# First feed-forward output product by seven quarter products, with the later weights' low halves alone rounded ahead and stored

## The chip, the cores and the metric

The kernel runs on one core of a Trainium2 chip. A core has a matrix engine (TensorE, PE in the profile, with PEld for its weight loads), two elementwise engines (VectorE, DVE; ScalarE, ACT), GpSimd (POOL), SyncE (SP) and 16 DMA engines, which are fed here by the queues of SP and of POOL. The engines run side by side and wait for each other by semaphores; each of them works off its own instructions in order. The metric is the device time in microseconds of one execution, as the median of several runs; less is better.

## The reference

A two-layer trunk over 512 tokens of width 1024, in float32:

```python
for layer in range(2):
    if layer == 0:   # state-space group and stick-breaking attention
        mix = concat(s5_mixer(u), attention(q, k, v)) @ mix_w_out + mix_b_out
    else:            # GLU, causal depthwise convolution (31 taps), layer norm, silu
        mix = conformer_conv(x, ...)
    x = layer_norm(4**0.25 * x + mix, ln1_g[layer], ln1_b[layer])
    ffn = square(relu(x @ ffn_w1[layer] + ffn_b1[layer])) @ ffn_w2[layer] + ffn_b2[layer]
    x = layer_norm(4**0.25 * x + ffn, ln2_g[layer], ln2_b[layer])
```

`ffn_w1` is 1024 x 4096 and `ffn_w2` 4096 x 1024: 32 tiles of 128 hidden features. The change is in layer 0's feed-forward, and in when the weights of what follows are prepared: the convolution's two pointwise products (`pw1`, 16 column tiles; `pw2`, 8) and the first six column tiles of layer 1's `ffn_w1`, 30 units of 128 columns in all.

## The kernel before

**Products.** TensorE multiplies in a rounded float format (`F32R`). To keep float32's precision every operand is split: `hi` is the value rounded (an ACT copy), `lo` the rest (`src - hi`, a DVE subtraction). A product is three matmuls: hi·hi, hi·lo, lo·hi (`gemm`, line 252). Activations lie feature by token: `X[0..7]`, each 128 features by 512 tokens, is the residual.

**Weights.** The class `Weights` (line 60) holds a list of units. `next()` (154) hands out the next one and first prepares as many as `ahead` tells: `fetch` (72) loads the raw block on SP's queue into one of two `raw` buffers, then lines 112 and 113 make `hi` and `lo` in one of the rotating slots. If `fence` is set, both are put behind an instruction of the layer norm. Where a stretch's pools are closed and others opened, the function `turn` (1322) does it, at a given unit.

**Layer 0's feed-forward** (1123) runs in four blocks of eight hidden tiles. `ffn1` (1080) makes the hidden tiles: 24 matmuls of 512 columns (`f`), relu on ACT, square on DVE, split. `accum` (844) multiplies by the block's `ffn_w2`: for each of eight output tiles 8 x 3 matmuls of 512 columns (`acf`), added to `X[j]`. The first six hidden tiles are computed half by half around the layer norm (`Lead`, `fl`). The fourth block's output product is the `Tail` (1008): 256 tokens at a time (`tlb`), so that the layer norm of one half lies under the product of the other. `tail_norm_lead` (1066) strings these together: tail, norm, then the first products of what follows (the lead; `pl` for the convolution).

**Kept units.** Between these products `W.keep` (142) prepares the 30 later units in full, raw load, `hi` and `lo`, and stores both to DRAM (`kepth`, `keptl`, SP's queue). In the convolution and its tail a unit of kind `split` (94) is just two loads on POOL's queue, `hi` and `lo`, with no compute engine.

**The convolution** (1134 to 1316) has its order written out by hand: `CONV_ORDER` lists steps (`g2`: GLU of tile 2, ending in the sigmoid `csg` on ACT and the gated input `hp` on DVE; `v`: taps on DVE; `p`: taps on PE; `M`, `Q`, `n`: norm). `in_order` (1225) chains all PE, DVE and ACT instructions that a step traces. Elsewhere the compiler orders each engine's instructions, by priority and by the times it expects.

**Layer 1's feed-forward** already uses seven products in place of eight for each 2 x 2 block product: blocks of six hidden tiles, `pair` (1369) turns two hidden tiles into seven combinations, `operand` (128) makes the seven combinations of the four quarters of `ffn_w2` (tiles `quad`, loaded by `load_quads`, 120), and `seven` (1386) runs the products (`s`), 512 wide because the residual is turned to token by feature there (`residual`, 1339). Its last block of eight is an ordinary product.

Of the kernel before, what the change touches and what calls it, by code (L numbers as in the profile page):

```python
# [16 lines left out]
P = 128  # L17
# [22 lines left out]
FFN_BLOCKS = ((8, 8, 8, 8), (6, 6, 6, 6, 8))  # L40
# [7 lines left out]
KEEP_FROM = 8  # L48
# [11 lines left out]
class Weights:  # L60


    def __init__(self, tc, ahead):
        self.tc, self.nc, self.ahead = tc, tc.nc, ahead
        self.slots, self.units, self.raw, self.urgent, self.fence, self.hold = [], [], None, True, None, False
        self.done, self.got, self.chunk, self.ready, self.kept = 0, 0, {}, {}, {}
        self.turn, self.quads, self.base = None, {}, 0
# [19 lines left out]
    def _prep(self, n):  # L87
        nc = self.nc
        while self.done < min(n, len(self.units)):
            key, src, nk, ncol, off, width = self.units[self.done]  # L90
            if self.turn and self.done == self.turn[0]:
                self.turn[1]()
            pool, s = self.slots[(self.done - self.base) % len(self.slots)]
            if key[0] == "split":
                w = tuple(pool.tile([P, nk, ncol], F32R, tag=f"w{x}{s}", name=f"w{x}{self.done}", bufs=1) for x in ("hi", "lo"))
                for x, d in zip(w, self.kept[key[1]]):
                    nc.gpsimd.dma_start(x, d)  # L97
                self.ready[self.done] = w
                self.done += 1
                continue  # L100
# [5 lines left out]
            hi = pool.tile([P, nk, ncol], F32R, tag=f"whi{s}", name=f"whi{self.done}", bufs=1)  # L106
            lo = pool.tile([P, nk, ncol], F32R, tag=f"wlo{s}", name=f"wlo{self.done}", bufs=1)
# [3 lines left out]
            else:  # L111
                i0 = nc.scalar.copy(hi, raw).ins  # L112
                i1 = nc.vector.tensor_sub(lo, raw, hi.bitcast(F32)).ins  # L113
            if self.fence:
                self.tc.add_manual_dep(i0, self.fence[0], NOSYNC, reason="behind the layer norm")
                self.tc.add_manual_dep(i1, self.fence[1], NOSYNC, reason="behind the layer norm")
# [24 lines left out]

    def keep(self, i):

        w = self.next()
        self.kept[i] = tuple(self.tc.dram_tile([P, *w[0].shape[1:]], F32, name=f"kept{x}{i}") for x in "hl")
        for x, d in zip(w, self.kept[i]):
            self.nc.sync.dma_start(d, x.bitcast(F32))
# [51 lines left out]
def kernel(ctx: ExitStack, tc: tile.TileContext, a: dict, out: bass.AP):  # L199
# [13 lines left out]
    X = [const([P, T], f"X{j}") for j in range(KT)]  # L213
# [49 lines left out]
    wst = ExitStack()  # L263
    wpool = wst.enter_context(tc.tile_pool(name="mw", bufs=1))
# [600 lines left out]
    wp2 = wst.enter_context(tc.tile_pool(name="w2", bufs=1))  # L865
    hst = ExitStack()
    hid = hst.enter_context(tc.tile_pool(name="hid", bufs=1, side="right"))
# [11 lines left out]
    def hpage(name, dt=F32R, w=T):  # L879
        return hid.tile([P, PAD + T + 2], dt, tag="hid", name=name, bufs=16)[:, :w]  # L880

    def tmp(name, dt=F32):
        return hid.tile([P, T], dt, tag="tmp", name=name, bufs=8)
# [6 lines left out]
    for j in range(0, D, 128):  # L890
        later += units_of("pw1", a["conv_w_pw1"][0], 0, 8, [j], 256)
        later += units_of("pw1", a["conv_w_pw1"][0], 0, 8, [D + j], 256)
    later += units_of("pw2", a["conv_w_pw2"][0], 0, 8, range(0, D, 128), 256)
    later += units_of("f1l", a["ffn_w1"][1], 0, 8, range(0, LEAD * P, 128), 256)

    kept = [k for j in range(0, 16, 4) for k in (j, j + 2, j + 1, j + 3)] + list(range(16, 24 + LEAD))
    keep_at, n = {}, 0
    for layer in range(2):
        if layer:
            units += [(("split", i), None, 8, 128, 0, 0) for i in range(24 + LEAD)]  # L900
            at_turn = len(W.units) + len(units)
        k0 = 0
        for nb in FFN_BLOCKS[layer]:
            if layer:
                units += units_of("f11", a["ffn_w1"][1], 0, 8, range(max(k0, LEAD) * P, (k0 + nb) * P, 128), 128)
                if nb == NB:
                    units += [(("quad", k0, i), None, nb // 2, T, 0, 0) for i in ORDER7]
                else:
                    for c in (0, T):
                        for k, n_ in ((0, 3), (3, 3), (6, 2)):  # L910
                            src = a["ffn_w2"][1][(k0 + k) * P : (k0 + k + n_) * P, c : c + T].rearrange("(k p) n -> p k n", p=P)
                            units.append((("f21", k0 + k, c), src, n_, T, 0, T))
                k0 += nb
                continue
            for m in range(k0, k0 + nb, 4):
                units += units_of("f10", a["ffn_w1"][0], 0, 8, range(m * P, min(m + 4, k0 + nb) * P, 128), 256)
                if m >= KEEP_FROM:
                    keep_at["f", m + 3] = kept[n : n + 2]
                    units += [later[i] for i in kept[n : n + 2]]
                    n += 2  # L920
            for j in range(0, KT, 4):
                units += units_of("f20", a["ffn_w2"][0], k0, nb, range(j * P, (j + 4) * P, 128), 256)
                if k0 + nb < 32:
                    m = 4 if j else 2
# [590 lines left out]
```

## Time and profile before

| | us |
|---|---|
| median of 3 runs (1159.39 to 1162.86) | 1160.79 |
| the profiled execution | 1164.9 |
| its span, first to last instruction | 1163.2 |

The mean granted TensorE clock was 0.994 of full. Durations in the text come from the profiled execution. The page's second part shows how its engines are used over time, in 40 slices of 29 us; each digit is a share in tenths:

```profile
PE   9989989999999999999999999999999999999997
DVE  7999865578645645645647699988695958588337
ACT  7857759435524524523513231364673536263530
DMA  9621212150878778788617634156024151515211
```

Layer 0's feed-forward lies in slices 11 to 20, the convolution in 22 to 26, layer 1's feed-forward from 30 on. In the views below, a row of instructions names engine, line, operation, the tile written and the tiles read (without buffer numbers), then count, busy time and mean duration. Matmul durations overlap, as they are pipelined; the distance from one start to the next tells how fast they run.

### The profile page before, as it was taken

To read this page: it belongs to the slowest core of one execution; us is meant where nothing else is said; L and a number is where in the kernel's file an instruction comes from. 1 tells how busy PE (TensorE), PEld (TensorE's weight loads), DVE (VectorE), ACT (ScalarE), POOL (GpSimd) and SP (SyncE) were. 2 spreads that over 40 slices of the span, in tenths; PEclk is the share of its full clock that TensorE was granted. 3 is DMA by queue.
4 is the path that set the end of the run, shared out by engine and by line. 5 is a ranking of instruction groups with operands and counts; after the bars stand their busy time and mean duration, and the time that the engine had idled before them with its cause. 6 is when DMAs were issued, how large, how long until landed. Compare 5 with 4: busy or idle time off the path is not lost.

```text
span 1163.2 us, 17835 instructions
## 1 busy us (share of the span) xinstructions
PE 1133.7 (97%) x7156; PEld 948.5 (82%) x7156; DVE 820.6 (71%) x1401; ACT 550.0 (47%) x838; POOL 70.2 (6%) x125
## 2 busy tenths in 40 slices
PE   9989989999999999999999999999999999999997
PEld 7777767799888888888899867689988888888885
DVE  7999865578645645645647699988695958588337
ACT  7857759435524524523513231364673536263530
POOL 1022221000000000000002211002000000000000
PEclk9999989999999999999999999999999999999999
DMA  9621212150878778788617634156024151515211
GB/s 204 173 63 50 74 56 74 55 181 14 267 244 289 250 273 282 267 268 274 217 46 245 226 137 146 39 170 227 4 82 135 50 151 44 172 35 156 65 54 73
DMA packets 145907, 169.59 MB, mean 146 GB/s; under 512 B 13922, under 2 KB 119138, under 8 KB 145824
## 3 DMA queue, kind: packets, MB, share of 16 engines
q1 hardware_dynamic: 137024, 136.96, 37.1%
q0 software_dynamic: 8640, 31.46, 8.0%
q8 instruction: 56, 0.92, 0.3%
q14 instruction: 27, 0.22, 0.1%
q10 hardware_dynamic: 160, 0.03, 0.0%
HBM read 132.12 MB, written 35.65 MB: 144 GB/s over the span
## 4 chain that ended last, share of the span: by engine, by line
PE 78%; DMA 6%; DVE 6%; ACT 5%; issue 2%; SPq 2%; POOL 1%; DVEq 0%; ACTq 0%
PE f L258 20%; PE acf L258 10%; PE s L1400 10%; DMA raw<-in_ffn_w_dram 4%; PE tld L258 4%; PE h L1445 4%; PE tlb L258 4%; PE fl L258 3%; PE pv L258 3%; PE cw L1174 3%; PE pg L258 3%; PE tla L258 2%; PE acmo L258 2%; DVE wlo L113 2%; PE pl L258 2%
## 5 line engine op out<-in xcount | busy, mean ns | idle before, releaser
L112 ACT CAST whi<-raw 128x1024 fp32r<-128x1024 f32 (+1 forms) x150 | 156.6, 1061 | 259.1 <-PE acf L258 66.3
L113 DVE TENSOR_TENSOR wlo<-raw,whi 128x1024 fp32r<-128x1024 f32 (+1 forms) x150 | 183.6, 1236 | 122.1 <-ACT whi L112 122.1
L258 PE MATMUL f<-xah,whi 128*128 128x512 f32 x208 | 81.0, 390 | 0.0
L258 PE MATMUL f<-xal,whi 128*128 128x512 f32 x208 | 81.0, 389 | 0.0
L258 PE MATMUL f<-xah,wlo 128*128 128x512 f32 x208 | 80.9, 389 | 0.0
L258 PE MATMUL f<-xdh,whi 128*128 128x512 f32 x208 | 80.9, 389 | 0.0
L258 PE MATMUL f<-xdl,whi 128*128 128x512 f32 x208 | 80.9, 389 | 0.0
L258 PE MATMUL f<-xdh,wlo 128*128 128x512 f32 x208 | 80.9, 389 | 0.0
L258 PE MATMUL acf<-hl,whi 128*128 128x512 f32 x192 | 75.8, 395 | 0.1
L258 PE MATMUL acf<-hh,wlo 128*128 128x512 f32 x192 | 75.7, 394 | 0.0
L258 PE MATMUL acf<-hh,whi 128*128 128x512 f32 x192 | 75.3, 392 | 0.0
L1400 PE MATMUL s<-whi,al 128*128 128x512 f32 x168 | 65.0, 390 | 0.0
L1400 PE MATMUL s<-wlo,ah 128*128 128x512 f32 x168 | 64.9, 390 | 0.0
L1400 PE MATMUL s<-whi,ah 128*128 128x512 f32 x168 | 64.5, 392 | 0.0
L113 DVE TENSOR_TENSOR wlo<-quad,whi 128x1536 fp32r<-128x1536 f32 x28 | 49.1, 1754 | 7.6 <-ACT whi L112 7.5
L391 DVE SCALAR_TENSOR_TENSOR cy<-hp,wdw,cy 128x512 f32<-128x512 f32 (+1 forms) x75 | 49.5, 660 | 0.5 <-ACT cy L187 0.5
L112 ACT CAST whi<-quad 128x1536 fp32r<-128x1536 f32 x28 | 41.0, 1483 | 17.2 <-PE f L258 8.0
L97 POOL DMA_DIRECT2D whi<-kepth x30 | 16.0, 535 | 547.6 <-PE tlb L258 386.7
L258 PEld LDWEIGHTS f<-xdh,whi 128*128 128x128 f32 x208 | 39.0, 188 | 8.1
L258 PEld LDWEIGHTS f<-xah,wlo 128*128 128x128 f32 x208 | 39.0, 188 | 8.1
L258 PEld LDWEIGHTS f<-xah,whi 128*128 128x128 f32 x208 | 39.0, 188 | 8.1
L258 PEld LDWEIGHTS f<-xdl,whi 128*128 128x128 f32 x208 | 39.0, 188 | 8.1
(647 smaller groups left out, 3064.4 us busy)
## 6 DMA issues: line engine op xcount, KB each, us to landing
raw<-in_ffn_w_dram SPq DMA_DIRECT2D x35, 1024.0 KB, 6.0
kepth<-whi SPq DMA_DIRECT2D x30, 512.0 KB, 4.4
keptl<-wlo SPq DMA_DIRECT2D x30, 512.0 KB, 9.5
whi<-kepth POOLq DMA_DIRECT2D x30, 512.0 KB, 3.6
wlo<-keptl POOLq DMA_DIRECT2D x30, 512.0 KB, 4.4
raw<-in_ffn_w_dram SPq DMA_DIRECT2D x28, 512.0 KB, 4.0
raw<-in_conv_w_pw_dram SPq DMA_DIRECT2D x12, 1024.0 KB, 6.7
quad<-in_ffn_w_dram SPq DMA_DIRECT2D x16, 768.0 KB, 4.6
```

The costliest lines, as they stand in the source:

```text
L97: nc.gpsimd.dma_start(x, d)
L112: i0 = nc.scalar.copy(hi, raw).ins
L113: i1 = nc.vector.tensor_sub(lo, raw, hi.bitcast(F32)).ins
L258: ins = PE.matmul(ps[:, c0:c1], u[:, k, ksl], v[:, c0:c1], start=start and k == 0 and i == 0, stop=stop and k == n - 1 and i == 2).ins
L391: V.scalar_tensor_tensor(o, x, s, y, op0=op0, op1=op1)
L1174: PE.matmul(cps[j, c0][g][C, :], Ds[j][t // 16][R, t % 16, :], hps[j][R, t + c0 : t + c1], start=t < 4, stop=t >= n - 4, tile_position=(R. ...
L1400: PE.matmul(ps, u, v[:, p, :], start=chain == i and p == 0 and n_ == 0, stop=p == len(As) - 1 and n_ == 2, skip_group_check=True)
L1445: PE.matmul(ps, u, v, start=k == 0 and i == 0, stop=k == nb_last - 1 and i == 2)
```

## The change

- **Layer 0's output product.** The first 24 hidden tiles run in four blocks of six with layer 1's scheme: `pair`, `load_quads`, `operand`, and a new `seven_by_feature`. Its results stay feature by token: a quarter (two feature tiles by 256 tokens) takes two matmuls of 256 columns where layer 1 has one of 512. Product 1 gathers in two pages `R1` over all blocks. The last eight hidden tiles are computed as before; their output weights are requested between them and the first four put into the memory of the quarters (`places`).
- **Residual.** `X` becomes one tile, is scaled ahead by eight ACT passes with its bias, and the tail only adds. Squares are taken on ACT.
- **Kept units.** `half_units` takes each later unit in two halves: load on POOL's queue into a page, ACT copy, DVE subtraction in place in the loaded page, store of the low half alone on POOL's queue. Each step first issues the load of the half two steps on. There are 60 steps: one per product, one per projection (none in the first block's, two each in the last block, one each from the seventh).
- **Later units.** A `split` unit is now a raw load on SP's queue, an ACT copy for `hi` (under the fence if one is set) and a load of `lo` on POOL's queue.
- **Pools.** Three turns (into layer 0's quarters, back to plain slots, into layer 1's quarters) reopen all pools in given orders; the tail's norm takes its temporaries from the 24 pages.

```diff
-FFN_BLOCKS = ((8, 8, 8, 8), (6, 6, 6, 6, 8))
+FFN_BLOCKS = (6, 6, 6, 6, 8)
...
-            if key[0] == "split":
-                w = tuple(pool.tile([P, nk, ncol], F32R, tag=f"w{x}{s}", name=f"w{x}{self.done}", bufs=1) for x in ("hi", "lo"))
-                for x, d in zip(w, self.kept[key[1]]):
-                    nc.gpsimd.dma_start(x, d)
...
                 i0 = nc.scalar.copy(hi, raw).ins
-                i1 = nc.vector.tensor_sub(lo, raw, hi.bitcast(F32)).ins
+                if key[0] == "split":
+                    i1 = nc.gpsimd.dma_start(lo, self.kept[key[1]]).ins
+                else:
+                    i1 = nc.vector.tensor_sub(lo, raw, hi.bitcast(F32)).ins
...
+        def load(n):
+            if n < 2 * n_kept:
+                (w, c), h = later[n // 2], n % 2
+                raws[n] = page(f"kr{n}")
+                G.dma_start(raws[n].bitcast(F32).rearrange("p (k n) -> p k n", k=4), w[4 * h * P : 4 * (h + 1) * P, c : c + P].rearrange("(k p) n -> p k n", p=P))
+
+        load(0)
+        load(1)
+        for n in range(2 * n_kept):
+            load(n + 2)
+            hi, raw = page(f"kh{n}"), raws.pop(n)
+            S.copy(hi, raw.bitcast(F32))
+            V.tensor_sub(raw, raw.bitcast(F32), hi.bitcast(F32))
+            G.dma_start(W.kept[n // 2][:, 4 * (n % 2) : 4 * (n % 2) + 4, :], raw.bitcast(F32).rearrange("p (k n) -> p k n", k=4))
+            yield
...
+    ORDERS = ("s1 s2 raw s3 a1 s4 a2 a0 q w", "s1 s2 raw w a1 s4 a2 b q s3 a0")
...
+    def seven_by_feature(k0, As, first, bi):
+        bank, opened = {}, None
+        for n, i in enumerate(ORDER7):
+            wh, wl = W.next()
+            chain = CHAIN.get(i, i)
+            for b in range(2):
+                if chain == i:
+                    bank[i, b] = nps(f"z{k0}{i}{b}")
+                ps = bank[chain, b]
+                for d in range(2):
+                    c = slice((2 * b + d) * P, (2 * b + d + 1) * P)
+                    for p, (ah, al) in enumerate(As):
+                        uh, ul = ah[:, PLACE[i]], al[:, PLACE[i]]
+                        for n_, (u, v) in enumerate(((wh, uh), (wh, ul), (wl, uh))):
+                            opens = chain == i and p == 0 and n_ == 0
+                            ins = PE.matmul(ps[:, d * H : (d + 1) * H], u[:, p, c], v, start=opens and d == 0,
+                                            stop=p == len(As) - 1 and n_ == 2, skip_group_check=True).ins
...
+                    tt(x, x, halves(ps), ALU.add)
+            keep()
...
+    for bi, nb in enumerate(FFN_BLOCKS[:-1]):
+        if bi:
+            W.load_quads(k0, a["ffn_w2"][0], k0, nb)
+        As = []
+        for m in range(k0, k0 + nb, 2):
+            As.append(pair(0, m, xs, first[m : m + 2] if bi == 0 else None, keep if bi else None))
+        seven_by_feature(k0, As, bi == 0, bi)
+        k0 += nb
+    hs, ws = [], []
+    for i in range(FFN_BLOCKS[-1]):
...
+        if i < 4:
+            ws.append(W.next())
+        x = region(i // 2, i % 2)
+        tt(x, x, halves(R1[i % 2]), ALU.add)
+        keep(2 - (i > 5))
```

More of the change, by code (lines that the diff above doesn't have):

```diff
@@ L47 @@
 ONE_SUM = "bd"
-KEEP_FROM = 8
 AHEAD = (5, 4)
@@ new lines, in plain, with in_quads @@
+    def plain():
+        wst[0].close()
+        wst[0] = ExitStack()
+        p = opened("tmp raw one hid four two three".split())
+        room.update(tmp=p["tmp"], hid=p["hid"], bufs=12)
+        W.slots, W.count, W.raw, W.ahead = [], 0, p["raw"], 5
+        for x, n in (("three", 3), ("two", 2), ("one", 1), ("four", 3)):
+            W.add_slots(p[x], n)
+    def in_quads(e):
+        return lambda n: tuple(f1["w"].tile([P, 8, P], F32R, tag=f"quad{e}{f}", name=f"w2{f}{n}", bufs=1) for f in range(2))
@@ L1121, in taps @@
         tt(mask, mask, ident[:, 96:], ALU.add)
[L1123 to L1131 removed]
+        yield
+    for j in range(KT):
+        act(X[j], X[j], AF.Identity, bias=rb[1][:, j : j + 1], scale=ALPHA)
```

301 lines of the change are left out of this document (167 added, 134 removed).

## The prediction

> **What bounds the kernel now.** I read the page first: engine totals, then the chain that ended last.
>
> ```profile
> PE 1133.7 (97%) x7156; PEld 948.5 (82%) x7156; DVE 820.6 (71%) x1401; ACT 550.0 (47%) x838; POOL 70.2 (6%) x125
> ...
> PE 78%; DMA 6%; DVE 6%; ACT 5%; issue 2%; SPq 2%; POOL 1%; DVEq 0%; ACTq 0%
> PE f L258 20%; PE acf L258 10%; PE s L1400 10%; DMA raw<-in_ffn_w_dram 4%; PE tld L258 4%; PE h L1445 4%; PE tlb L258 4%; PE fl L258 3%; PE pv L258 3%; PE cw L1174 3%; PE pg L258 3%; PE tla L258 2%; PE acmo L258 2%; DVE wlo L113 2%; PE pl L258 2%
> ```
>
> TensorE leads, and `acf`, the first layer's output product outside its last block, is a tenth of the chain. An average hides stages, so next the busy times by stretch: the first feed-forward (301.5 to 577.7), its tail (to 625.6), the convolution (650 to 764).
>
> ```profile
> core 0: us, PE busy (x) PEld busy (x) DVE busy (x) ACT busy (x) POOL busy (x), PEclk, DMA share, GB/s
> 301.50:577.70 276.20, 276.11 (x1211) 225.82 (x1210) 148.53 (x165) 113.79 (x134) 0.00 (x0) 1.00 0.79 270
> 577.70:625.60 47.90, 46.96 (x390) 46.56 (x389) 29.43 (x68) 9.98 (x22) 7.55 (x14) 1.00 0.41 140
> 650.00:764.00 114.00, 110.36 (x1609) 80.63 (x1611) 106.05 (x198) 37.48 (x71) 13.73 (x26) 1.00 0.41 137
> ```
>
> In the first stretch PE never rests, while DVE works 54% and ACT 41%: there only TensorE work counts, and DVE or ACT work saved buys nothing. In the convolution PE (97%) and DVE (93%) both bind, so a wait put on either one is paid.
>
> **Term 1, the product itself.** The column after the length is PE's busy time of `acf` alone; below it starts of 512-wide and of 256-wide matmuls.
>
> ```profile
> 301.00:578.00 277.00, 134.12 (x576) 108.05 (x576) 16.47 (x24) 1.00 0.79 270
> ...
> 577.72 0.28 PE L258 MATMUL tlb<-hh,whi 128*128 128x256 f32 x1
> ...
> 578.55 0.28 PE L258 MATMUL tlb<-hl,whi 128*128 128x256 f32 x1
> ...
> 577.00:626.00 49.00, 46.91 (x384) 46.20 (x384) 7.34 (x16) 1.00 0.41 140
> ...
> 854.00:1069.00 215.00, 115.88 (x504) 94.06 (x504) 35.70 (x54) 1.35 (x2) 1.00 0.36 109
> ```
>
> Removed: 24 hidden tiles x 8 output tiles x 3 = 576 matmuls in 134.1 us, 0.233 each. Added: 4 blocks x 7 products x 3 pairs x 3 parts x 4 quarter tiles (b, d) = 1008 matmuls, 256 wide, because the layer stays feature by token. The two `tlb` starts lie seven steps apart: 0.83/7 = 0.1186 us. The whole `tlb`, waits included, gives 46.91/384 = 0.1222 (row two). I take 0.120, nearer to the undisturbed steps: 121.0 us, a gain of **13.1 us** (ends 14.6 and 10.9). The second layer does the same seven products 512 wide, 504 in 115.9 us (row three); the narrow form costs about 5 us more than that.
>
> The Trainium skill, "TensorE: Matmul & The Clock Gate", section "Back-to-back issue gap", has N/2.4 + 2.5 ns, 216 and 109 ns; by it the gain would be 576 x 0.216 - 1008 x 0.109 = 14.5 us. The trace has 233 and 119, so I keep the rows.
>
> **Term 2, cover inside the blocks.** Layer 1 already runs this pattern. Its product phase, projection phase and last block:
>
> ```profile
> 883.50:916.10 32.60, 32.60 (x145) 26.99 (x144) 21.02 (x23) 17.09 (x20) 0.00 (x0) 1.00 0.22 62
> 916.10:945.00 28.90, 28.90 (x128) 23.55 (x127) 24.65 (x27) 11.95 (x12) 0.00 (x0) 1.00 0.51 149
> ...
> 1068.00:1111.00 43.00, 43.00 (x192) 35.59 (x191) 17.00 (x17) 22.00 (x29) 0.00 (x0) 1.00 0.32 103
> ...
> L248 ACT CAST hh<-fr 128x512 fp32r<-128x512 f32 x28 | 17.3, 619 | 24.7 <-DVE fr L387 24.7
> ...
> L249 DVE TENSOR_TENSOR hl<-fr,hh 128x512 fp32r<-128x512 f32 x27 | 18.6, 689 | 11.7 <-ACT hh L248 11.7
> ```
>
> Each of the 60 kept halves adds one 512-wide ACT copy (0.62) and one DVE subtraction (0.69). A product phase gets seven: DVE 24.65 + 4.8 = 29.5 of 252 x 0.120 = 30.2 us; ACT 16.3. A projection phase gets six: DVE 25.2 of 32.6; ACT 20.8. So it fits, with nothing to spare in the product phase; a lag is buffered by three prepared weights and six PSUM banks, and drains in the projection phase. I cost it at 0.5; without that cover DVE would set the phase, at 10% over some 2 us a block, 9 in all. Residual scaling (eight ACT passes), squares and the operands' differences lie under the same cover, as they do in layer 1.
>
> **Start of block 0.** Layer 1 covers the first quarter weights with its transposes, which layer 0 lacks:
>
> ```profile
> L1346 PE MATMUL xt<-ident,X 128*128 128x128 f32 x32 | 3.8, 274 | 0.0
> ...
> L113 DVE TENSOR_TENSOR wlo<-quad,whi 128x1536 fp32r<-128x1536 f32 x28 | 49.1, 1754 | 7.6 <-ACT whi L112 7.5
> ...
> L112 ACT CAST whi<-quad 128x1536 fp32r<-128x1536 f32 x28 | 41.0, 1483 | 17.2 <-PE f L258 8.0
> ```
>
> Slot s1 opens on memory that the fifth and sixth lead weights hold; the sixth is read until 301.5. Its high half lies under the fifth, free 2.9 us sooner, so the cast (1.48) is out in time and the subtraction (1.75) comes after 301.5. Until then PE has 16 products of high weights from two finished pairs, 1.9 us. Between 0 and 3.2; I take **1.5**.
>
> **The last block.** Here layer 0 has what layer 1 has not: 8 projection and 8 output weights plus 14 halves in 8 x 5.44 = 43.5 us.
>
> ```profile
> L112 ACT CAST whi<-raw 128x1024 fp32r<-128x1024 f32 x81 | 83.1, 1049 | 122.0 <-PE acf L258 66.3 <-DMA raw<-in_ffn_w_dram 33.8 <-DMA raw<-in_conv_w_pw_dram 11.8
> ...
> q1 hardware_dynamic: 32440, 27.21, 36.2%
> ...
> q1 hardware_dynamic: 51331, 74.57, 78.4%
> ```
>
> ACT: 22.0 + 8 x 1.05 + 14 x 0.62 = 39 us at most; DVE 17 + 8 x 1.22 + 14 x 0.69 = 36. DMA: 16 x 0.524 + 14 x 0.524 = 15.7 MB. The queue rows are of 860 to 1110 and of 301 to 580: 27.21 MB in 36.2% of 250 us is 301 GB/s with 512-byte rows, 74.57 MB in 78.4% of 279 us is 341 with wider ones. Four output weights (2.1 MB) may land during the tail, so 13.6 MB, 40 to 45 us. All three are close to the block's length. Halves are two steps ahead, here only 5.4 us, and six free pages carry loads, stores and activations. A late load holds ACT's queue, behind it the relu, and with two projection banks PE. From 0 to 8 (all 15.7 MB at 301 GB/s is 52 us); I take **2.5**.
>
> The second norm: five of the later weights are cast before its lead; the three or so that fall among its squares and outputs add 1.05 each to ACT. PE has the second half of the tail meanwhile; before, only this was left over:
>
> ```profile
> PE pl L258 <- ACT xbh L187: 0.3, 1, 0.3
> ```
>
> 0 to 3, I take **0.5**.
>
> **The convolution.** A later weight used to need no compute engine; now it needs an ACT cast, and `in_order` nails ACT's order there. At step `g2`, two requests with five ahead put the casts of units 6 to 10 in front of tile 2's sigmoid `csg`.
>
> ```profile
> 651.74 0.71 ACT L187 ACTIVATE cz<-hp,wdw 128x512 f32<-128x512 f32 x1
> 661.18 0.69 ACT L193 ACTIVATE csg<-pg,PV 128x512 f32<-128x512 f32 x1 [8.74 <-PE pg L258]
> ...
> 659.21 0.08 DVE L1157 MEMSET hp<- 128x30 f32 x1
> 661.91 0.75 DVE L391 SCALAR_TENSOR_TENSOR hp<-pv,PV,csg 128x512 f32<-128x512 f32 x1 [2.62 <-ACT csg L193]
> ...
> raw<-in_ffn_w_dram SPq DMA_DIRECT2D x26, 512.0 KB, 4.0
> ```
>
> Only two raw buffers exist. From 652.4: units 6, 7 are there (cast to 654.5); unit 8's load starts at 653.5 and takes 4.0 (last row), 9 follows 1.0 later; casts to 659.7; unit 10's load starts at 658.7, its cast ends at 663.9. The sigmoid moves from 661.2 to 663.9, and DVE, already waiting there, waits 2.7 us more. Queued behind the casts on ACT are `csg`, then the start of tile 1's taps; behind DVE's wait all later taps, up to the sums of the convolution's norm. DVE's few gaps (about 1 us until 752) absorb little: **2.0**, from 0 (units landing early) to 6 (loads slowed to 6 us by the low halves). From `g3` on each step needs two casts in 11 us, hidden.
>
> The second layer's tail gets nine casts, 9.5 us, on an ACT that works about half of it: **0.5** (0 to 3). Not paid: the old 30 full casts and subtractions and the old 31 MB of stores, which the first stretch hid. Layer 1's blocks keep their operations.
>
> **Sum.** -13.1 + 0.5 + 1.5 + 2.5 + 0.5 + 2.0 + 0.5 = -5.6 us. The profiled execution took 1164.9 (span 1163.2 plus 1.7): 1159.3. The three runs' median is 1160.8, 4.1 lower: **1155**.
>
> **Rivals.**
> *All hidden.* The compiler puts low-priority copies into ACT's 23 us of idle in the tail, and nothing waits: -13.1 + 0.5 = 1148. For it: layer 1 loses almost nothing at its phase changes. Against: ACT's order in the convolution is fixed. Chance 0.13.
> *Given back.* Last block 5, block 0 3, convolution 4, others 2: +14, net about +1, 1161. For it: the tight shares above. Chance 0.23.
> *Slower: the halves' loads set the pace.* POOL issues them in order with the stores.
>
> ```profile
> L97 POOL DMA_DIRECT2D wlo<-keptl x24 | 12.9, 537 | 0.2 <-issue 0.2
> ```
>
> That is a load of 128 rows of 4 KB; a half has 512 rows of 512 B, unseen on this queue: between 0.54 and four times that, 2.1 us. At 2.1, loads and stores take 14 x 2.7 = 37 us of POOL in the last block, and a load needs about 2.1 + 4 to land, over the 5.4 us of two steps. It decides where the issue exceeds about 1.5 us and the stores do not free pages in time: then each ACT copy waits 0.3 to 1 us, some 20 of them in the product phases and all in the last block, 34 x 0.7 = 24 us; 1155 + 24 - 2.5 = 1176. Against: two steps are 8.6 us in product phases. Chance 0.20.
> The Trainium skill, "DMA: Bandwidth & Descriptors", section "Measured (HBM→SBUF, 128 partitions, SWDGE, issued from GpSimd)", asks for at least 1 MiB per transfer. Its fit in "Anatomy of one DMA", 2.0 us plus bytes/436e3, estimates 2.6 us per half, which would be in time; no run here shows such a half.
>
> **Chances.** Forecast 1149 to 1159: 0.44; all hidden 0.13; given back 0.23; slower 0.20. A measurement tells 0.3% (3.5 us) from no change: 1157.3 and 1164.3. Most of the forecast (0.42) and all hidden fall below: faster 0.55; same 0.24, mostly given back; slower 0.21. The range, 1147 to 1168, leaves out the far end of the slower case and a little below.
>
> **What would show it.** Term 1: 1008 matmuls at L-lines of `seven_by_feature`, about 121 us; over 124 refutes it. Block 0: PE idle before its first low-weight product. Last block: its eight projections longer than 43.5 us, with ACT waiting for DMA. Convolution: tile 2's `csg` near 664 less the time gained before it, DVE idle in front of it. Wrong from the start if 256-wide matmuls run slower beside 200 GB/s of transfers than in the tails.

## The result and the profile after

| | before | after |
|---|---|---|
| median of the runs, us | 1160.88 | 1203.56 (1197.36 to 1205.13) |
| profiled execution / its span, us | 1164.9 / 1163.2 | 1203.2 / 1201.5 |

The ratio is 1.0357, with a 95% interval of 1.0317 to 1.0396: slower by 3.6%, where 0.5% faster was forecast. From the page of the changed kernel, its engine totals, PE and the granted clock by slices, and the chain that ended last:

```profile
PE 1144.3 (95%) x7588; PEld 973.1 (81%) x7588; DVE 898.1 (75%) x1505; ACT 629.7 (52%) x944; POOL 128.0 (11%) x215
...
PE   9889999999998989899999999999999999999997
...
PEclk9989999999899998999999999999999999999999
...
PE 55%; DVE 10%; DMA 8%; issue 7%; ACT 6%; POOL 3%; SPq 0%; DVEq 0%; POOLq 0%; ACTq 0%
```

TensorE's share of the chain fell from 78% to 55%, although it has more matmuls. In slices 11 to 20, where PE had only nines, three are eights now, and so are two of the clock's. DVE (75%) and ACT (52%) are far from full, so the time is in waits. Measured from the start of one tile's work to the start of the next, in microseconds of the one profiled execution of each kernel:

| stretch | before | after | forecast change | measured change |
|---|---|---|---|---|
| blocks of the first feed-forward (end of `fl` to first `tlb`) | 276.1 | 299.8 | -8.6 | **+23.7** |
| its tail | 47.8 | 48.2 | 0 | +0.4 |
| lead of the convolution (`pl`) | 24.7 | 29.9 | +0.5 | **+5.2** |
| convolution | 114.3 | 115.9 | +2.0 | +1.6 |
| second layer's tail, to the first `fl` on its norm | 51.2 | 56.2 | +0.5 | **+5.0** |
| second feed-forward, from its first transpose to the first `h` | 260.3 | 264.6 | 0 | +4.3 |
| all else (mixer, leads, end) | 388.8 | 386.9 | 0 | -1.9 |

What TensorE, ACT and POOL waited for in the blocks (the largest rows of the view of waits; in total, times, longest):

```profile
PE f L254 <- ACT q L182: 12.0, 4, 3.4
PE z L1239 <- ACT ah L1120: 4.7, 3, 2.7
```
```profile
ACT kh L911 <- DMA kr<-in_conv_w_pw_dram: 30.7, 14, 4.7
...
ACT kh L911 <- DMA kept<-kr: 22.0, 14, 3.5
```
```profile
POOL kr L904 <- DMA kept<-kr: 54.0, 23, 5.0
```

Read from below: POOL's loads of halves wait for stores to land, because the page they want is still being stored; ACT's rounding copies (`kh`) wait for those loads, or for a page themselves; TensorE waits for the relu (`q`) and the combinations (`ah`) that ACT has not done. All rows of TensorE in the blocks sum to 21.2 us, where the kernel before had none, and stretches at half clock (last section) cost 11.9 us more. Less the 13.1 us that the product gains, that is 20.0 of the 23.7. One such moment, on ACT and on TensorE:

```profile
362.88 0.61 ACT L911 CAST kh<-kr 128x512 fp32r<-128x512 f32 x1
367.00 0.62 ACT L911 CAST kh<-kr 128x512 fp32r<-128x512 f32 x1 [3.50 <-DMA kept<-kr]
367.52 1.47 ACT L110 CAST whi<-quad 128x1536 fp32r<-128x1536 f32 x1
368.90 0.68 ACT L182 ACTIVATE q<-f,PV 128x512 f32<-128x512 f32 x1
```
```profile
366.49 0.39 PE L254 MATMUL f<-xah,wlo 128*128 128x512 f32 x1
369.63 0.51 PE L254 MATMUL f<-xah,whi 128*128 128x512 f32 x1 [2.75 <-ACT q L182]
```

The copy waits 3.50 us for a page; the relu, two places behind it, comes at 368.90, and TensorE, with both projection banks full, stands for 2.75 us.

Where the copies run is the second thing to see. Busy time of the copies alone (line 911), by phase. The first row is the projections of the second block; the rows behind the gap are projections and products of the third block, then of the fourth; the last row is the last block.

```profile
core 0: us, ACT busy (x), PEclk, DMA share, GB/s
...
340.30:375.90 35.60, 6.79 (x11) 0.95 0.71 221
...
407.80:448.80 41.00, 7.43 (x12) 0.96 0.75 225
448.80:484.60 35.80, 3.72 (x6) 0.90 0.60 192
484.60:522.30 37.70, 3.08 (x5) 0.95 0.53 167
522.30:553.90 31.60, 0.00 (x0) 1.00 0.21 61
553.90:597.80 43.90, 7.96 (x13) 1.00 0.84 250
```

The diff traces six copies in each projection phase and seven in each product phase. The compiler, which orders ACT here, pulled copies ahead: 11 (one straddles the edge) and 12 in the first two projection phases, none in the last product phase. Such a phase needs 32.7 us for the 144 matmuls of its six hidden tiles. The first took 35.6 us with 10 starts, although nine of its matmuls (2.0 us) had run ahead among the first block's products; the second took 41.0 with 12. That is about 3.5 us for each half.

### The profile page after: what moved, and what is told of

It is laid out like the page before. It is cut to its first block, busy times and chain, and to the rows that moved or that the text cites. A ratio compares the mean times of both kernels' runs of the same rounds, so it can differ in the third digit from the quotient of the medians.

```text
span 1201.5 us, 19145 instructions
## 1 busy us (share of the span) xinstructions
PE 1144.3 (95%) x7588; PEld 973.1 (81%) x7588; DVE 898.1 (75%) x1505; ACT 629.7 (52%) x944; POOL 128.0 (11%) x215
## 4 chain that ended last, share of the span: by engine, by line
PE 55%; DVE 10%; DMA 8%; issue 7%; ACT 6%; POOL 3%; SPq 0%; DVEq 0%; POOLq 0%; ACTq 0%
PE f L254 13%; PE s L1507 10%; PE fl L254 4%; PE z L1239 4%; PE tld L254 4%; PE h L1552 4%; DMA raw<-in_conv_w_pw_dram 2%; DMA raw<-in_ffn_w_dram 2%; PE tlb L254 2%; PE cw L1327 2%; PE tla L254 2%; ACT whi L110 2%; DVE cy L388 2%; PE acmo L254 2%; DVE wlo L114 2%
## 5 line engine op out<-in xcount | busy, mean ns | idle before, releaser
L110 ACT CAST whi<-raw 128x1024 fp32r<-128x1024 f32 (+1 forms) x122 | 128.8, 1062 | 201.9 <-PE s L1507 47.8
L114 DVE TENSOR_TENSOR wlo<-raw,whi 128x1024 fp32r<-128x1024 f32 (+1 forms) x92 | 114.5, 1247 | 85.7 <-ACT whi L110 85.6
L114 DVE TENSOR_TENSOR wlo<-quad,whi 128x1536 fp32r<-128x1536 f32 x56 | 98.1, 1754 | 10.0 <-ACT whi L110 9.1
L1239 PE MATMUL z<-ah,whi 128*128 128x256 f32 x336 | 96.1, 294 | 8.4 <-ACT ah L1120 4.7
L110 ACT CAST whi<-quad 128x1536 fp32r<-128x1536 f32 x56 | 82.2, 1481 | 37.6 <-PE z L1239 15.1
L1239 PE MATMUL z<-al,whi 128*128 128x256 f32 x336 | 97.1, 291 | 1.0 <-DVE al L1121 0.9
L1239 PE MATMUL z<-ah,wlo 128*128 128x256 f32 x336 | 96.5, 290 | 0.0
L1239 PEld LDWEIGHTS z<-ah,whi 128*128 128x128 f32 x336 | 66.1, 200 | 10.2 <-ACT ah L1120 5.5
L911 ACT CAST kh<-kr 128x512 fp32r<-128x512 f32 x60 | 37.0, 617 | 70.8 <-DMA kr<-in_conv_w_pw_dram 30.7
L912 DVE TENSOR_TENSOR kr<-kr,kh 128x512 fp32r<-128x512 f32 x60 | 41.3, 688 | 37.7 <-ACT kh L911 37.7
L1239 PEld LDWEIGHTS z<-al,whi 128*128 128x128 f32 x336 | 66.9, 199 | 1.7 <-DVE al L1121 1.6
L1239 PEld LDWEIGHTS z<-ah,wlo 128*128 128x128 f32 x336 | 66.9, 200 | 0.0
L1121 DVE TENSOR_TENSOR al<-q,ah 128x768 fp32r<-128x768 f32 (+1 forms) x48 | 52.2, 1089 | 12.2 <-ACT ah L1120 12.2
```

What stands on the lines that cost most here:

```text
L911: S.copy(hi, raw.bitcast(F32))
L912: V.tensor_sub(raw, raw.bitcast(F32), hi.bitcast(F32))
L1121: V.tensor_sub(lo, src, hi.bitcast(F32))
L1239: ins = PE.matmul(ps[:, d * H : (d + 1) * H], u[:, p, c], v, start=opens and d == 0, stop=p == len(As) - 1 and n_ == 2, skip_group_check=T ...
```

## The experiments

Each is the changed kernel with the edit shown (the last two change the kernel before); times are medians, the ratio is to the kernel before. The length of a stretch is that of one profiled execution: `best_a`, which holds the edit of `store_sp` and one more, came out 3.9 us longer there, so differences of a few microseconds between two versions are not sure.

**Parts alone.** `no_halves` takes the 60 steps out:

```diff
-            next(half_unit, None)
+            (one store in all; no load, copy or subtraction)
```


> Leaves out the 60 half steps (load, copy, subtraction, store); every later unit's low half is read from one block of DRAM written once. Theory A (the half steps hold ACT's queue, PE waits and its clock is halved after each wait): the four blocks and the last block, 299.7 us in the changed kernel from the end of the lead to the first tail product, fall to 264 to 270, and the kernel to 1167 to 1175. Rival B (the seven products 256 wide, their operands and the 512 KB loads are slow by themselves): the stretch stays above 288 and the kernel above 1190.

Measured 1177.41 us, ratio 1.0134 (1.0112 to 1.0157), blocks 274.3: most of the way to theory A, but 4 us short of its range. The halves cost 25.5 us of the blocks: TensorE's waits there fall from 21.2 to 5.2 us and what the half clock takes from 11.9 to 3.4, 24.5 together, so a third of the price is the clock. By phase, without and with the halves (the nine matmuls that ran ahead counted with their projections): first products 36.8 and 39.3; projections 32.7, 32.7, 32.7 and 37.6, 41.0, 37.7; later products 31.6, 31.6, 31.8 and 31.9, 35.8, 31.6; last block 43.5 and 43.9. So 13 of the 25.5 us lie in the two projection phases with the bunches and 12 in three phases next to them. In the last of these three, the fourth block's projections, copies wait 9.9 us for loads; in the third block's products it is a wait of 2.73 us for `ah`, around which TensorE had half its clock for 6.8 us. Almost nothing lies in the last block, where I had put it.

`no_store` leaves out the halves' stores (but the first unit's):

```diff
-            G.dma_start(W.kept[n // 2]..., raw...)
+            if n < 2: G.dma_start(W.kept[0]..., raw...)
```


> Leaves out the stores of the low halves but for the first two; loads, copies and subtractions stay. Theory A1 (pages are held until a store has landed, and copies and loads wait for pages): ACT's 22 us and POOL's 54 us of waiting for stores go, the stretch of 299.7 us falls to 275 to 285, the kernel to 1180 to 1190. Theory A2 (the loads themselves, two steps ahead, land too late, or the copies and subtractions are too much for ACT and DVE): the stretch stays at 293 or more, the kernel above 1196.

1189.21 us, 1.0241 (1.0205 to 1.0277), blocks 284.8, the upper edge of the first range. 15 of the 25.5 us come from stores, which hold pages; with pages freed at once, 15 or 16 copies fit into a projection phase of 33 to 35 us, 2.2 us each.

`hi_by_dma` loads the later units' raw blocks straight into the place of their high parts, with no cast, and `whole_units` keeps whole units as before in place of halves:

```diff
-    hi = S.copy(raw);  lo = load(kept)
+    hi = load(raw block, not rounded);  lo = load(kept)            # hi_by_dma
-    60 halves by pages
+    30 whole units by the weight slots, hi and lo stored on SP's queue   # whole_units
```


> A later unit's high half is loaded raw into its slot by POOL's queue, so its rounding on ACT is left out; all else as in the changed kernel. Theory C (casts that wait for raw loads hold ACT's queue in the second norm, in the convolution and in the second tail): the lead after the second norm falls from 29.9 to 25, the convolution from 116.0 to 114.5, the second layer's tail from 56.2 to 51.5; the kernel to 1190 to 1194. Rival D (temporaries in pages and the new order of the pools do it): all three stay within 1 us, the kernel within 3 us of 1203.6.

> Only the first part of the change: seven quarter products in layer 0; the later units are prepared whole in the weight slots, both halves stored by SP's queue and loaded by POOL's, as before the change, 30 of them between the products at every second step. Theories A and C: blocks 264 to 274 us, lead, convolution and second tail as before the change, the kernel 1150 to 1162, which would beat 1160.9 or equal it. Rivals B and D: 1180 or more.

`hi_by_dma`: 1194.45 us, 1.0289 (1.0259 to 1.0318); lead 24.7, convolution 114.0, second tail 49.9: theory C. The casts of the later units cost 5.2 + 1.9 + 6.3 = 13.4 us; 6.7 come back at the start of the second feed-forward, where the transposes now wait. Why they do was not followed. `whole_units`: 1197.25, 1.0299 (1.0269 to 1.0329); blocks and tail 347.0 against 348.0 after and 323.9 before. The 1150 to 1162 of theories A and C did not come. Lead and second tail are back (24.7 and 50.9), but the old way of keeping does no better beside the seven products: TensorE waits 14.0 us there for the casts and low parts of weights (`whi`, `wlo`). So queue and pages of the halves are not the only way to lose these 24 us; what else this version lacks was not followed. What a cast did in the second norm, on ACT in the changed kernel, and then a window of 25 us on TensorE's lead in `hi_by_dma` (busy time of PE, PEld, DVE, ACT, POOL, then granted clock, DMA share and GB/s):

```profile
639.63 1.05 ACT L110 CAST whi<-raw 128x1024 fp32r<-128x1024 f32 x1 [8.08 <-DMA raw<-in_conv_w_pw_dram]
640.59 0.47 ACT L188 ACTIVATE rb<-vpb,cb 128x256 f32<-128x256 f32 x1
```
```profile
646.00:671.00 25.00, 24.74 (x194) 24.06 (x193) 14.95 (x38) 10.68 (x22) 9.66 (x14) 1.00 1.37 269
```

The third cast stands ahead of the norm's reciprocal root and waits 8.08 us for a load. Its own 1.05 us, which I had counted, is the small part.

**The product by itself.** `product_only` joins `no_halves` and `hi_by_dma`; `product_pairs` also changes the order within each block's first product:

```diff
-    for b: for d: for each of three pairs
+    for the first two pairs over all b, d; then the third pair over all b, d     # first product only
```


> Left out: the rounding and storing of the later weights' low halves; later units load high and low parts as they are kept, with no cast (so the later products' numbers are meaningless). What stays of the change is the seven products, the early scaling and the pools. Theory (the product pays little even alone): no_halves gave 1177.4 with the blocks at 274.3, 1.8 less than before; taking the casts away gave back 5.2 in the convolution's lead, 1.9 in the convolution and 6.3 in the second layer's tail (run hi_by_dma against after). So 1177.4 - 13.4 = 1164, and 1171 if the transposes at the start of the second feed-forward wait as they did in hi_by_dma; stretch of the blocks 272 to 276. Rival (the prediction's first term is all gained once nothing else is added): blocks 263 to 265, time 1148 to 1154.

> product_only with the first product of each block taking two pairs over all quarter tiles before the third. Left out as there: rounding and storing of the later low halves and the casts of the later units. Theory M (the third pair's low part, awaited 0.9 us in each block, and the low clock after it are what is left): the 3.5 us of waits for al and 1 us for ah go, blocks 268 to 271, time 1162 to 1166. Rival N (the wait moves to the next weights): blocks 273 to 275, time 1167 to 1170. In neither case is the predicted gain of 13 there: before's blocks take 276.1.

1168.49 us, 1.0066 (1.0049 to 1.0084), blocks 274.1; and 1166.00, 1.0058 (1.0037 to 1.0079), blocks 271.1. TensorE's largest row of waits in the blocks, first of `product_only`, then of `product_pairs` (whose other two rows are 0.3 and 0.2):

```profile
PE z L1250 <- DVE al L1132: 3.5, 4, 0.9
```
```profile
PE z L1253 <- ACT whi L118: 2.2, 3, 1.0
```

The first lies between its two ends, 1164 and 1171; the second is at the edge of theory M: each block had waited 0.9 us for its third pair. What is left, 2.7 us of waits and 3.4 lost to the low clock, is in block 0: its products take 36.7 us against 30.6 in each later block, which is the 1008 x 0.120 / 4 = 30.2 of the forecast. `pairs_outer`, the same reordering in the changed kernel:

> The first of the seven products of each block takes its first two pairs over all four quarter tiles before the third pair: 24 matmuls, 2.9 us, before the third pair is wanted, in place of 6, 0.7 us. Theory E (part of the loss is the third pair's combination that comes too late, 4.7 us for ah and 0.9 for al, each wait followed by a stretch at half clock): blocks fall by 6 to 12, time 1191 to 1198. Rival F (the wait only moves to the next product's weights or to the projections): blocks fall by under 2, time 1200 to 1204.

1201.50 us, 1.0367 (1.0339 to 1.0395), blocks 296.6: 3.2 less in the stretch, between both theories, and no clear difference in time. `best_a`, the same with stores on SP's queue (below):

> Stores on SP's queue and the first product's pairs in the other order, together. If the two add (12.3 and 3.2 us of the blocks): blocks 283 to 286, time 1185 to 1189. If the waits that the second removes are the same: blocks 287 to 289, time 1189 to 1193. Neither comes near the kernel before.

1193.92 us, 1.0277 (1.0248 to 1.0306), blocks 291.4, above both ranges and no better than `store_sp`: no sign that the two add.

**Which engine does the halves.**

```diff
-            S.copy(hi, raw);  V.tensor_sub(raw, raw, hi)
+            G.tensor_copy(hi, raw);  G.tensor_sub(raw, raw, hi)      # halves_pool
+            V.tensor_copy(hi, raw);  V.tensor_sub(raw, raw, hi)      # copy_dve
```


> Copy and subtraction of each half on GpSimd in place of ACT and DVE; loads and stores as they are. Theory A (an ACT copy that waits for its load or its page holds the relu, square and cast queued behind it, and with two projection banks TensorE): those waits leave ACT, the blocks fall from 299.8 to 276 to 283, time 1180 to 1188. Rival B (what costs is the transfers and the pages that they hold, whichever engine waits): blocks 292 to 300, time 1195 to 1205. Rival C (GpSimd is too slow: loads 0.75, stores 0.56 and two passes of perhaps 1.2 each are 3.7 us a half where a product lasts 4.3, and it shares DVE's way to memory): the halves lag behind, the last block and the tail wait, time over 1205.

> The rounding copy of each half on DVE in place of ACT, nothing else. Theory A (head of the queue: whichever engine holds the copy waits for the load, and what is behind it waits too): DVE's queue holds the combinations, the low weights and the sums of the products, so the loss stays, blocks 295 to 305, time 1198 to 1208, with TensorE's waits named after DVE. Rival D (ACT's own load is the point, 34 us of copies on it): blocks fall by 10 or more, time under 1192.

`halves_pool`: 1229.05 us, 1.0594 (1.0564 to 1.0623), blocks 322.3; rival C, and by the last of its reasons: DVE became slow beside POOL (last section). `copy_dve`: 1206.36, 1.0392 (1.0351 to 1.0433), blocks 306.0: no gain, as theory A said, its blocks 1 us above the range. DVE now waits 35.6 us for pages, ACT waits for DVE's combinations, and TensorE still waits for `q`, which theory A had not said:

```profile
DVE kh L911 <- DMA kept<-kr: 35.6, 17, 6.2
```
```profile
ACT ah L1120 <- DVE q L384: 40.9, 9, 9.6
```
```profile
PE f L254 <- ACT q L182: 10.3, 4, 4.8
```

In the changed kernel ACT's row was 5.5 us. Of the two engines, whichever holds the copy passes the wait on. ACT's load is not the point.

**Pages, loads, stores, order.**

```diff
-            load(n + 2)
+            load(n + 1)                                     # one_ahead
-            G.dma_start(W.kept[n // 2]..., raw...)
+            nc.sync.dma_start(W.kept[n // 2]..., raw...)    # store_sp
-            S.copy(hi, raw);  V.tensor_sub(raw, raw, hi)
+            the same two, each under a priority lower by 120 instructions   # later120
```


> Loads of the halves one step ahead in place of two. Theory A (ACT's copies wait for their loads): a load takes 5.1 us from issue to landing, a product phase's step 4.3, so the copies wait longer, blocks 303 to 312, time 1206 to 1216. Rival P (pages are what is short; a load in flight less gives one back to the stores and copies): blocks 288 to 296, time 1191 to 1200.

> The halves' stores on SP's queue in place of POOL's, nothing else. Theory G (a store is issued behind a load that itself waits for a page; the page of that store is then late too): POOL's waits of its loads for stores, 54 us, shrink and with them the copies' waits for pages, blocks 288 to 295, time 1191 to 1198. Rival H (each store waits for its subtraction at the head of SP's queue, and the weights' loads behind it come late): ACT's waits for raw loads grow, blocks over 303, time over 1206. No change: 298 to 302.

> The copy and the subtraction of each half are given to the compiler with a priority some 120 instructions (about one product and a half) lower; work, pages, loads and stores are the same. On ACT each copy then stands one to two places further back, behind a weight's cast, a relu or a square that stood behind it before. Theory A (what costs is that copies stand in ACT's queue ahead of the weights' casts and the hidden tiles, at a place where their load or page has not come yet): TensorE's waits for q and ah shrink, blocks 285 to 292, time 1188 to 1195. Rival B (the transfers and the pages set the pace, the place in the queue does not matter): blocks 297 to 304, time 1200 to 1207.

`one_ahead`: 1210.18 us, 1.0412 (1.0384 to 1.0440), blocks 301.9: theory A's time. Rival P was half right: with one load less in flight ACT's waits for stores to leave a page nearly went (22.0 to 4.6 us), but its waits for loads rose by more (30.7 to 58.6 us, of which 44.7 from the one array):

```profile
ACT kh L910 <- DMA kr<-in_conv_w_pw_dram: 44.7, 20, 5.3
...
ACT kh L910 <- DMA kept<-kr: 4.6, 2, 2.6
```

`store_sp`: 1190.61 us, 1.0263 (1.0233 to 1.0293), blocks 287.5: theory G, a little below its ranges. POOL's timeline of the changed kernel shows what SP's queue avoids:

```profile
350.31 0.56 POOL L913 DMA_DIRECT2D kept<-kr  x1
353.32 0.75 POOL L904 DMA_DIRECT2D kr<-in_conv_w_pw_dram  x1 [2.45 <-DMA kept<-kr]
354.06 0.56 POOL L913 DMA_DIRECT2D kept<-kr  x1
356.95 0.75 POOL L904 DMA_DIRECT2D kr<-in_conv_w_pw_dram  x1 [2.33 <-DMA kept<-kr]
357.69 0.56 POOL L913 DMA_DIRECT2D kept<-kr  x1
```

A load waits for a store to land, and the next store stands behind that load: stores follow each other by 3.6 to 3.8 us. In the trace, 28 of the 60 stores were issued more than 0.5 us after their subtraction had ended (74 us in sum, 6.7 the longest); on SP's queue none was. The store itself is not faster there (last number, median from issue to landing; after, then `store_sp`, where the trace has the landing of 16 of the 60):

```profile
kept<-kr POOLq DMA_DIRECT2D x60, 256.0 KB, 4.8
```
```profile
kept<-kr SPq DMA_DIRECT2D x60, 256.0 KB, 5.1
```

`later120`: 1203.24 us, 1.0365 (1.0337 to 1.0393), blocks 298.6: rival B's numbers. The lower priority changes nothing, and the bunches stay (12 copies in each of the first two projection phases, none in the last products). The next edit removes the bunches: it ties each copy, on ACT, behind the weight's cast traced last before it.

```diff
-            S.copy(hi, raw.bitcast(F32))
+            tc.add_manual_dep(S.copy(hi, raw.bitcast(F32)).ins, W.last, NOSYNC, reason="in turn")
```


> Each half's copy is tied, on ACT alone, behind the weight's cast that was traced last before it, so that the compiler can no longer pull it ahead: six halves in a projection phase and seven in a product phase, in place of 10, 12 and 5, and 6, 6 and 0. Theory Q (the halves run at 3.4 us each through POOL's queue and the pages; ten or twelve of them in a projection phase of 32.7 us make it 36 to 41): those phases come back to 33 to 34, blocks 278 to 285, time 1181 to 1188. Rival R (where the copies stand does not matter, as later120 said): blocks 295 to 302, time 1198 to 1206.

> The same with the stores on SP's queue. Theory Q: once the halves are spread, 4.3 to 5.4 us are there for each, so the store's place adds little: blocks 275 to 281, time 1178 to 1184. Rival R: as store_sp, blocks 286 to 289, time 1189 to 1193.

> The same again with the first product's pairs in the other order, which product_pairs showed to be worth 3 us of the blocks where nothing else disturbs them: blocks 272 to 278, time 1175 to 1181. Even then the casts of the later units (13.4 us by hi_by_dma) are still paid, so it should not beat the kernel before.

`spread`: **1187.27 us**, 1.0214 (1.0176 to 1.0251), blocks 280.9, 18.9 less with the same work, pages, loads and stores: theory Q. Copies in the last two blocks of six and in the last block:

```profile
402.90:435.50 32.60, 3.66 (x6) 1.00 0.54 174
435.50:467.10 31.60, 4.32 (x7) 1.00 0.74 233
467.10:499.80 32.70, 3.65 (x6) 1.00 0.58 178
499.80:530.90 31.10, 4.31 (x7) 1.00 0.45 143
530.90:580.20 49.30, 7.93 (x13) 0.97 0.87 260
```

Projection phases with six copies are back at 32.7, and the last two product phases with seven at 31.1 to 31.6. (Among the second block's products eight ran, and these took 34.0.) The last block, at 49.3, now pays 5.8, with one wait of 3.8 us for a relu (`r`). `spread_sp`: 1181.46, 1.0172 (1.0141 to 1.0204), blocks 279.6; `spread_sp_pairs`: 1185.26, 1.0187 (1.0151 to 1.0224), blocks 277.7. The blocks came out as theory Q has them, the time of the last 4 us above its range (of which 3 in the mixer, which no edit touches). The three versions lie too close together to rank them; none beats the kernel before.

**Waits and the clock.** In the kernel before, copies that the relu overwrites were put ahead of it at the last hidden tile of three blocks:

```diff
+            for _ in range({7: 6, 15: 9, 23: 14}.get(m, 0)): S.copy(r, ps)      # stall_before
+            for _ in range({7: 16, 15: 18, 23: 22}.get(m, 0)): S.copy(r, ps)    # clock_stall
```


> The kernel before, with three delays put on ACT ahead of the relu of the last hidden tile of the first three blocks of the first feed-forward: 6, 9 and 14 idle copies of 0.66 us of the same tile, overwritten by the relu. The output is the same. The next product needs that tile; some 2.3 us of delay are hidden as before, so TensorE should wait about 1.7, 3.6 and 6.9 us, 12.2 in all. Theory K (a wait of TensorE of a microsecond or more is followed by a stretch of 3.4 us at half clock, which costs 1.7 more): three such stretches where the profile of before has none in the blocks, time 1160.9 + 12.2 + 5.1 = 1178. Rival L (the low clock in the changed kernel comes from its other activity, not from waits): no such stretch, time 1173.

> stall_before with 16, 18 and 22 idle copies of 0.585 us in place of 6, 9 and 14. There 8.2 us of delay left a wait of 0.7, so 7.5 are hidden; waits of about 1.9, 3.0 and 5.4 us are to be expected, 10.3 in all. Theory K (a wait of TensorE of some 2.5 us or more is followed by a stretch at half clock): stretches of 3.4 us after the second and third wait, 1.7 us each, time 1160.8 + 10.3 + 3.4 = 1174.5. Rival L (the low clock comes from something else that the changed kernel does): no stretch, time 1171.

1163.45 us, 1.0028 (1.0011 to 1.0045), with waits of 0.7 us at most; and 1168.42, 1.0077 (1.0062 to 1.0092), with waits of 1.31 and 2.29 us. Neither shows a stretch at half clock in the blocks, which is what rival L has. The delays were hidden better than reckoned, so a wait of over 2.5 us was never made, and theory K is not settled by them.

## Why the prediction was wrong

**Term 1, the product: right.** 1008 matmuls start 0.120 us apart, and undisturbed later blocks took 30.6 us against 30.2. The waits among them are other terms.

**Term 2, "cover inside the blocks", at 0.5: the step that failed.** Its capacity sum was sound (in the view beside it the first row is the projection phase and the second the product phase, the other way round than its heading says; the sum takes them rightly): with the copies where the diff traces them, two product phases with seven halves each took 31.1 and 31.6 us (`spread`). Two things were wrong. It took the traced order for the one that runs, though the description of the kernel says that the compiler orders ACT here; the copies ran in bunches of 10 to 12. And it summed the busy times of ACT and DVE, not the loop that a half goes round: load, copy, subtraction, store, page free, with loads and stores in one in-order queue, some 3.5 us a half. `no_halves` measures the term at 25.5 us (0.4 of it in the last block), of which 8.5 are stretches at half clock, which no term had. 18.9 of the 25.5 go with the bunching (`spread`), 12.3 with the stores' place in POOL's queue (`store_sp`); the two overlap, as both together (`spread_sp`) gain only 20.2. Term 2 also took layer 1's pattern as covered; here each block's first product waited 0.9 us for its third pair, and `product_pairs` gained 3.0 us by another order.

**Start of block 0, 1.5 (0 to 3.2): too small.** With nothing else added it took 36.7 - 30.6 = 6.1 us (`product_pairs`): 2.2 us of waits, of which 0.63 and 1.02 for the high parts of weights, where the prediction looked for a low part, and two stretches at half clock behind them, 1.7 us each. The waits were within the range, the clock was not thought of.

**The last block, 2.5 (0 to 8): right place only when the halves are spread.** It cost 0.4 in the changed kernel, 5.8 in `spread`. The forecast looked there for the pace of the halves and left the product phases out.

**Second norm and second tail, 0.5 each: mis-sized by ten times**, 5.2 and 5.0. The casts were counted by their own length. In the norm, three of them waited 11.9 us for raw loads (8.08 in one place) and held the norm behind them. In the second tail they stood among the passes that TensorE needed: it waited 1.8 us for `csh`, and a half clock behind that took 1.7; the rest of the 5.0 is not traced.

**Convolution, 2.0: right**, 1.6 measured, and by the way that was told. Tile 2's sigmoid came behind its casts, and DVE waited 5.82 us for it in place of 2.62, where 2.7 more were forecast; DVE's gaps made up for the rest:

```profile
691.67 0.75 DVE L388 SCALAR_TENSOR_TENSOR hp<-pv,PV,csg 128x512 f32<-128x512 f32 x1 [5.82 <-ACT csg L188]
```

**Layer 1's blocks "keep their operations"**: they do, but 1.4 us of waits at the transposes and first products and a slower pitch (`s` 231 instead of 227 ns, `f` 228.5 instead of 226.7, some 2.8 us together) made 4.3 us. What moved the pitch stays open.

**The rivals.** The slower one said that each copy would wait 0.7 us on the average, 24 us in all, 1176. The sum of the halves, 25.5, came out; its reason only in part, so the number is partly luck. Of its two conditions, that stores do not free pages in time came true; a POOL issue of over 1.5 us did not. The issue took 0.75, and it is the waiting load in front of the store, not the issuing, that fills the queue. Nor did the last block pay, where it had 14 of its 34 waits. The estimate of 2.6 us for a half, which the prediction worked out from the Trainium skill, "DMA: Bandwidth & Descriptors", section "Anatomy of one DMA", is half of what the trace has for 48 of the 60 loads, beside other traffic:

```profile
kr<-in_conv_w_pw_dram POOLq DMA_DIRECT2D x48, 256.0 KB, 5.1
```

**The sum.** Even with all later-weight work left out the kernel is slower than before, 1166 to 1168 us. In `product_pairs` block 0 takes 6.1 of the 13.1 us, and the second feed-forward 10.5 (waits of 5.3 us at the transposes and 3.4 lost to the clock), where the changed kernel loses 4.3: the blocks alone, at 271.1 against 276.1, do gain 5.0.

## What to carry to other kernels

Work that "fits under" a busy engine has to fit phase by phase, in the order that the compiler makes, not in the order of the source: count its instructions by phase in the trace, and tie background work to the step it belongs to. Follow a background item once round its whole loop (load, compute, store, buffer free): a queue that holds both the load waiting for a buffer and the store that frees one sets the pace. An instruction put on an in-order engine costs the wait of its operand too, not its own length alone.

## What the runs showed of the hardware

**Stretches at half clock follow waits of TensorE.** The windows of the changed kernel around the moment shown above (busy time of PE, PEld, DVE, ACT, POOL, then granted clock, DMA share and GB/s):

```profile
367.00:370.00 3.00, 0.37 (x2) 0.32 (x3) 1.52 (x1) 2.97 (x4) 1.29 (x2) 1.00 0.48 172
370.00:373.40 3.40, 3.40 (x10) 2.63 (x9) 3.13 (x4) 3.37 (x5) 0.00 (x0) 0.50 0.07 28
373.40:383.00 9.60, 8.55 (x56) 7.60 (x54) 9.60 (x12) 6.16 (x9) 2.59 (x4) 1.00 0.29 94
```

After 2.75 us of waiting the clock is 0.50 for 3.4 us. In the blocks of the changed kernel there are six such stretches (one of them double), 11.9 us lost; in those of before, none. Over all 20 traces, from 296 to 860 us, waits that stand alone (no other of 0.4 us or more begins within 8 us) were followed by such a stretch, begun during the wait or within 2.5 us of its end, so often:

| length of the wait, us | followed | of |
|---|---|---|
| 0.4 to 1 | 0 | 38 |
| 1 to 2 | 5 | 30 |
| 2 to 2.5 | 11 | 13 |
| over 2.5 | 22 | 25 |

This is a count, not an experiment. The longest wait that was made on purpose, 2.29 us in `clock_stall`, stood alone and was not followed: it is one of the two exceptions in the third row. So that waits are the cause is not shown. The Trainium skill, "TensorE: Matmul & The Clock Gate", section "HAM oscillation — how this bites in real kernels", warns of idle gaps above some 3.4 us. Here gaps from 2 us on mostly go with it, and several shorter ones close together, as in block 0.

**GpSimd's passes slow DVE's two-input passes.** The same DVE instructions, after and, with POOL's subtraction, in `halves_pool`:

```profile
L384 DVE TENSOR_TENSOR q<-q 128x256 f32<-128x256 f32 x39 | 16.4, 420 | 1.9 <-ACT q L182 1.8
```
```profile
L912 POOL TENSOR_TENSOR kr<-kr,kh 128x512 fp32r<-128x512 f32 x52 | 80.9, 1555 | 1.3
...
L384 DVE TENSOR_TENSOR q<-q 128x256 f32<-128x256 f32 x39 | 38.8, 995 | 0.4
```

420 ns became 995 in the mean. Within `halves_pool`, the 14 of the 39 that ran beside no pass of POOL took 417 to 426 ns, the ten beside its rounding copy alone 824 to 1036, and the 15 beside its subtraction 823 to 1992. DVE's sums into `X`, whose second input lies in PSUM, stayed at 680 ns in both kernels. The Trainium skill, "SBUF — State Buffer", section "Who interferes with whom", has it that a DVE instruction with two inputs in SBUF contends with a GpSimd instruction that reads SBUF; the trace agrees.
